# A hybrid decoder step: all low parts of the split weights on DVE, and one more slot in the mLSTM heads between the power and the row scaling

## Chip, cores and metric

One core of a Trainium2 chip. The metric is the time of one execution on the device in microseconds (us), as the median of several runs. All times below are of the core's engines as the hardware profiler recorded them: PE (TensorE, matrix products; PEld its weight loads), DVE (VectorE), ACT (ScalarE), POOL (GpSimd) and SP (SyncE, which issues DMAs).

## The reference, cut to what matters

One layer of a decoder runs on 512 prompt tokens and 64 sample tokens (8 sequences of 8), with a width of 1024 and fp32 throughout:

```
hn = rmsnorm(x) * (1 + sc1) + sh1                      # adaLN from c
u  = hn @ w_in
z, xbc, dt, q, k, v, o, ig, fg, xr, gr = split(u)
y_ssd = rmsnorm(ssd_chunked(silu(conv(xbc)), softplus(dt), ...) * silu(z))
y_ml  = rmsnorm(mlstm_chunked(q, k, v, ig, log_sigmoid(fg))) * sigmoid(o)
y_lru = lru_scan(...) * gelu(gr)
x  = x + g1 * (concat(y_ssd, y_ml, y_lru) @ w_out)
h2 = rmsnorm(x) * (1 + sc2) + sh2
x  = x + g2 * (relu(h2 @ w_up)**2 @ w_down)
y  = rmsnorm(x)                                         # and 14 state outputs
```

`ssd_chunked` goes through 128-token chunks of 16 heads in two groups; `mlstm_chunked` does the same for 4 heads and ends in `num / max(|den|, exp(-m))`, whose rows are then RMS-normalised per head.

## The kernel before

The 576 tokens are the free axis of every product, in two halves of 288. The weights are cut into 125 blocks of 1024 x 128. So that fp32 products can be made of three faster ones, each block is split as it arrives: a high part `wh`, the weight rounded to fp32r by ACT (L150), and a low part `wl`, the raw weight minus the high part (L152). The activations are split likewise, and `mm_k` (L164) makes hi x hi, hi x lo and lo x hi for two halves and eight k: 48 products of about 0.13 us, some 6.4 us of PE per block. Blocks have buffers for three raw tiles, three high and three low parts (`RAW_BUFS`, `W_BUFS`); raw tiles are loaded four blocks ahead and split two blocks ahead (`LOOKAHEAD`, `PREP`).

Which engine makes the low part is set by `WL_POOL`: blocks 7 to 32 on POOL, all others on DVE. In the trace POOL's 26 start between 68.0 and 345.6 us. The products of a block gather in a PSUM slot (`pg`, two slots); an evacuation follows, which for the twelve conv blocks (`ev_conv`, L605 to L653) is: ACT copies the sums into a row buffer `r` (L611 to L614; four such buffers), ACT and DVE do the four taps (L620, L626), ACT a tanh (L649), and DVE the gate into `xbc` (L651, L653), which also ends the use of the row buffer.

Between the blocks runs everything else, as Python generators: the gate rows, two SSD groups (`ssd`), four mLSTM heads (`mlstm`), the RG-LRU, the adaLN rows, the gates. `unit` gives each generator in `active` a step (`slot()`) after every four of a block's eight k, which is every 24 products, and after its end. A `yield` therefore means "the next instructions are written one slot later". The order of blocks is written out (`ORDER`: conv blocks c9 c11 c4 c5 c6, mLSTM head m0, c7, m1, m2, then z, x, g and o blocks, m3 late). The order in which each engine finally gets its instructions is not this order: the framework's scheduler reorders the program by a simulated timeline, so that another engine for one instruction moves others on every engine.

In an SSD chunk, L688 to L691 make `cb` and `xt` on PE, DVE makes `cbm` (L693), `xdt` and `xend` (L698) and `att` (8 x L707, ACT's exp, 2 x L711), and PE makes `py` (L729, from the second chunk on also L732) and the state product `ps` (L734). DVE then writes y from `py` (4 x L736). In an mLSTM head, `mlstm` ends with column work: DVE to L1053, the power -1/2 on POOL (L1054), a product (L1056) and the scaling of five row tiles `num` (L1059); after a slot PE transposes them into `pt` (L1063, L1064), and ACT copies them out.

Of the kernel before, what the change touches and what calls it, by code (L numbers as in the profile page):

```python
# [22 lines left out]
FT = mybir.dt.float32  # L23
# [3 lines left out]
OP = mybir.AluOpType  # L27
# [40 lines left out]
class Kernel:  # L68
# [63 lines left out]
    def w_prep(self, upto):  # L132
        nc = self.nc
        while self.w_next_split <= min(upto, NBLK - 1):
            b = self.w_next_split
            self.w_load(b)
            raw = self.w_raw.pop(b)
            m = raw.shape[2]
            if b == 0:
                self.w_split[b] = raw  # L140
            elif b == 3:
                hl = [[self.T("wt", FR)[:, :512].rearrange("p (k m) -> p k m", k=4) for _ in range(2)] for _ in range(2)]
                for (hi, lo), src in zip(hl, (raw[:, :4], raw[:, 4:])):
                    nc.scalar.activation(hi, src, AF.Copy)
                    nc.vector.tensor_tensor(lo, src, hi.bitcast(FT), op=OP.subtract)
                self.w_split[b] = (lambda k, t=hl: t[k // 4][0][:, k % 4], lambda k, t=hl: t[k // 4][1][:, k % 4], m)
            else:
                hi = self.wpool.tile([128, 8, m], FR, name=self.name("wh"), tag="wh", bufs=W_BUFS)
                lo = self.wpool.tile([128, 8, m], FR, name=self.name("wl"), tag="wl", bufs=W_BUFS)
                nc.scalar.activation(hi, raw, AF.Copy)  # L150
                eng = nc.gpsimd if b in WL_POOL else nc.vector
                eng.tensor_tensor(lo, raw, hi.bitcast(FT), op=OP.subtract)  # L152
                self.w_split[b] = (lambda k, t=hi: t[:, k], lambda k, t=lo: t[:, k], m)
            self.w_next_split += 1

# [749 lines left out]
    def mlstm(self, h, q, k, v):  # L905
        nc, io = self.nc, self.io
# [145 lines left out]
        nc.vector.tensor_tensor(ss, ss, r2, op=OP.mult)  # L1052
        nc.vector.tensor_scalar(ss, ss, 1.0 / 128, EPS, op0=OP.mult, op1=OP.add)  # L1053
        nc.gpsimd.tensor_tensor(r2, ss, self.mhalf, op=OP.pow)  # L1054
        fac = cp()
        nc.vector.tensor_tensor(fac, den, r2, op=OP.mult)  # L1056
        for c in range(5):
# [422 lines left out]
W_BUFS = 3  # L1480
RAW_BUFS = 3
CONV = "addd"
WL_POOL = range(7, 33)
ON_POOL = ('fin', 's0', 'S', 'rmax', 'gu1', 'gu2', 'cf2', 'vm')
TAIL = 2, 1, 2

# [152 lines left out]
```

## Time and profile before

| what | value |
|---|---|
| median of 3 runs | 996.15 us (993.74, 996.48, 996.15) |
| the profiled execution | 995.4 us, of which its span 993.6 us |
| mean granted clock of PE | 0.987 |
| PE busy | 959.5 us, 97% of the span |
| DVE busy | 590.2 us, 59% |
| ACT busy | 399.8 us, 40% |
| POOL busy | 203.8 us, 21% |

The profile is of one execution, and its times are counted from the span's start. A group of instructions is told by its line, its engine, its operation and its tiles, `out<-in`. A wait is put down to the instruction that ended it, as in "PE g L164 <- ACT r L614". A matrix product's row gives how long it took with its neighbours overlapping it, so that one of 0.13 us is shown with more. The clock column of a stretch is the clock that PE was granted there, 1.00 being full speed.

### The profile page before, as it was taken

The page shows a single profiled execution, that of the slowest core. Times are in us where ns is not written, and L with a number is a line of the kernel's source. Part 1 is how long each engine was busy: PE and PEld are TensorE (multiplying, and loading weights), DVE is VectorE, ACT ScalarE, POOL GpSimd, SP SyncE. Part 2 cuts the span into 40 slices and gives each one's busy share as a digit, 9 for nine tenths or more (in the row PEclk, how much of TensorE's full clock was granted, in tenths as well). Part 3 has the DMA queues.
Part 4 walks back from the last instruction along what each step waited for, and adds up shares of the span by engine and source line. Part 5 has one row for each costly group of instructions (what it writes and reads, how often), then busy time and mean ns, then how long its engine had stood idle before and what let it go on. Part 6 is the DMA issues. An engine that isn't in the chain of part 4 may idle for free.

```text
span 993.6 us, 18146 instructions
## 1 busy us (share of the span) xinstructions
PE 959.5 (97%) x7369; PEld 904.1 (91%) x7370; DVE 590.2 (59%) x1180; ACT 399.8 (40%) x741; POOL 203.8 (21%) x220
## 2 busy tenths in 40 slices
PE   8999789889999999999999999999999999999996
PEld 5889778777788899999999999999999999999996
DVE  4669897887788377468444455533553355335544
ACT  3454744453646674345222234312441144114320
POOL 2836454532355532020000000000000000000032
PEclk8999999998999999999999999999999999999998
DMA  9721254654464333444222322222222222222202
GB/s 343 294 86 64 81 186 133 246 173 137 131 223 153 105 137 129 140 131 162 91 98 105 110 86 84 74 79 84 85 86 85 86 85 76 76 83 85 85 23 96
DMA packets 51220, 119.62 MB, mean 120 GB/s; under 512 B 6956, under 2 KB 17468, under 8 KB 51136
## 3 DMA queue, kind: packets, MB, share of 16 engines
q1 hardware_dynamic: 47024, 111.06, 32.7%
q10 hardware_dynamic: 3744, 6.85, 1.8%
q8 instruction: 58, 0.95, 0.4%
q0 software_dynamic: 368, 0.55, 0.2%
q14 instruction: 26, 0.21, 0.1%
HBM read 108.68 MB, written 9.76 MB: 119 GB/s over the span
## 4 chain that ended last, share of the span: by engine, by line
PE 76%; DVE 10%; ACT 4%; issue 3%; DMA 1%; POOL 0%; POOLq 0%; DVEq 0%; ACTq 0%
PE g L164 66%; DVE r L626 3%; PE adap L218 1%; PE g L1363 1%; DMA nmb<-scr_nm 1%; PE py L729 1%; PE lg L1129 1%; DVE att L707 1%; PE ps L734 1%; PE py L732 1%; DVE nmb L924 1%; DVE xbc L651 0%; DVE sp_e L494 0%; PE adas L228 0%; ACT r L620 0%
## 5 line engine op out<-in xcount | busy, mean ns | idle before, releaser
L150 ACT ACTIVATE wh<-raw 128x1024 fp32r<-128x1024 f32 x123 | 130.1, 1058 | 333.9 <-PE g L164 309.4
L164 PE MATMUL g<-hnh,wh 128*128 128x288 f32 x688 | 153.1, 302 | 10.1 <-ACT r L614 8.0
L164 PE MATMUL g<-hnh,wl 128*128 128x288 f32 x688 | 152.1, 299 | 0.6 <-DVE wl L152 0.6
L164 PE MATMUL g<-hnl,wh 128*128 128x288 f32 x688 | 151.8, 299 | 0.0
L152 DVE TENSOR_TENSOR wl<-raw,wh 128x1024 fp32r<-128x1024 f32 x97 | 118.7, 1225 | 29.5 <-ACT wh L150 29.4
L164 PEld LDWEIGHTS g<-hnh,wh 128*128 128x128 f32 x688 | 110.4, 189 | 19.3 <-ACT r L614 9.2
L164 PEld LDWEIGHTS g<-hnh,wl 128*128 128x128 f32 x688 | 111.6, 189 | 2.7 <-issue 1.2
L164 PEld LDWEIGHTS g<-hnl,wh 128*128 128x128 f32 x688 | 111.7, 189 | 0.8 <-issue 0.4
L164 PE MATMUL g<-h2h,wh 128*128 128x288 f32 (+1 forms) x512 | 110.9, 297 | 0.0
L164 PE MATMUL g<-h2l,wh 128*128 128x288 f32 (+1 forms) x512 | 110.9, 298 | 0.0
L164 PE MATMUL g<-h2h,wl 128*128 128x288 f32 (+1 forms) x512 | 110.0, 296 | 0.0
L307 DVE SCALAR_TENSOR_TENSOR xr<-g,modt,xr 128x288 f32<-128x288 f32 x38 | 19.7, 518 | 141.2 <-PE g L164 141.2
L164 PE MATMUL g<-hh,wl 128*128 128x288 f32 x480 | 102.9, 295 | 0.0
L164 PE MATMUL g<-hh,wh 128*128 128x288 f32 x480 | 102.5, 295 | 0.0
L164 PE MATMUL g<-hl,wh 128*128 128x288 f32 x480 | 102.4, 295 | 0.0
L1405 POOL TENSOR_SCALAR xr<-xr,vec 128x576 f32<-128x576 f32 (+2 forms) x8 | 15.2, 1900 | 383.8 <-ACT sqa L1237 363.4
L152 POOL TENSOR_TENSOR wl<-raw,wh 128x1024 fp32r<-128x1024 f32 x26 | 69.0, 2653 | 80.3 <-ACT wh L150 61.4
L164 PEld LDWEIGHTS g<-h2h,wl 128*128 128x128 f32 x512 | 83.4, 188 | 0.0
L164 PEld LDWEIGHTS g<-h2h,wh 128*128 128x128 f32 x512 | 83.1, 189 | 0.1
L164 PEld LDWEIGHTS g<-h2l,wh 128*128 128x128 f32 x512 | 83.0, 188 | 0.0
L164 PEld LDWEIGHTS g<-hh,wh 128*128 128x128 f32 x480 | 77.0, 188 | 0.0
L164 PEld LDWEIGHTS g<-hh,wl 128*128 128x128 f32 x480 | 77.0, 188 | 0.0
(399 smaller groups left out, 1652.7 us busy)
## 6 DMA issues: line engine op xcount, KB each, us to landing
raw<-w SPq DMA_DIRECT2D x124, 512.0 KB, 3.5
ada<-ada SPq DMA_DIRECT2D x32, 512.0 KB, 5.6
ada<-ada SPq DMA_DIRECT2D x32, 256.0 KB, 5.9
cumb<-scr_cum SPq DMA_DIRECT2D x16, 256.0 KB, 5.6
s<-s SPq DMA_DIRECT2D x16, 256.0 KB, 4.7
ssm_s<-s ACTq DMA_DIRECT2D x16, 256.0 KB, 2.9
x<-x SPq DMA_DIRECT2D x8, 288.0 KB, 4.7
xr<-x SPq DMA_DIRECT2D x8, 288.0 KB, 3.9
```

The source lines that it names most:

```text
L150: nc.scalar.activation(hi, raw, AF.Copy)
L152: eng.tensor_tensor(lo, raw, hi.bitcast(FT), op=OP.subtract)
L164: self.nc.tensor.matmul(pg.h[h][:m, :e], w(k), xx[:, h * HALF:h * HALF + e], start=start and n == 0, stop=stop and n == 2)
L218: nc.tensor.matmul(ps[32 * j:32 * j + 32, :256], self.cs[:, k, :], ks(k), start=k < 4, stop=k >= 4)
L307: self.nc.vector.scalar_tensor_tensor(dst[:, :HALF], pg.h[0][:, :HALF], gate[:, 0:1], x[:, :HALF], op0=OP.mult, op1=OP.add)
L626: nc.vector.scalar_tensor_tensor(a[:, :n], r[:, j:j + n], wcols[:, j:j + 1], a[:, :n], op0=OP.mult, op1=OP.add)
L707: self.eng("att").tensor_scalar(E[:, h * 128:(h + 1) * 128], cums[h2][:, h * 128:(h + 1) * 128], self.col1[:, c, hd:hd + 1], 0.0, op0=OP.a ...
L729: nc.tensor.matmul(o, xdt[:, h * 64:(h + 1) * 64], att[h // 4][:, hs], start=True, stop=not c)
L732: nc.tensor.matmul(o, S[:, h * 64:(h + 1) * 64], ce[h // 4][:, hs], start=False, stop=True)
L734: nc.tensor.matmul(pst, cb[:, 128:256], xend[:, :512], start=True, stop=True)
L924: self.eng("nmb").tensor_scalar(E[:, tk(c)], nmb[:, tk(c)], ecol(c), 0.0, op0=OP.add, op1=OP.min)
L1405: self.eng("fin").tensor_scalar(x, x, self.v("fnw")[:, o:o + 1], None, op0=OP.mult)
```

## The change

`WL_POOL` is gone: the low part of every block is made on DVE (26 instructions of L152 move from POOL to DVE). In each of the four heads a `yield` stands between the power on POOL and the product and scaling on DVE, so that the latter two are written a slot later, and the transposes with them. Nothing else in the code is changed. In the rows below, the lines 152 to 1053 of the kernel before are one lower; lines 1056 to 1064 are the same.

```
@@ w_prep
                 nc.scalar.activation(hi, raw, AF.Copy)
-                eng = nc.gpsimd if b in WL_POOL else nc.vector
-                eng.tensor_tensor(lo, raw, hi.bitcast(FT), op=OP.subtract)
+                nc.vector.tensor_tensor(lo, raw, hi.bitcast(FT), op=OP.subtract)
@@ mlstm
         nc.gpsimd.tensor_tensor(r2, ss, self.mhalf, op=OP.pow)
+        yield
         fac = cp()
         nc.vector.tensor_tensor(fac, den, r2, op=OP.mult)
@@
-WL_POOL = range(7, 33)
```

The scheduler's new order, at three places. The first is PE's, at the first two chunks of the first SSD group: `py_1434` is the first chunk's product, `py_1563` the second's, and g_1724 is the block of weights between them. Before:

```order
L729 MATMUL py_1434<-att_1372,xdt_1368 64x128 x4
L729 MATMUL py_1434<-att_1379,xdt_1368 64x128 x4
L734 MATMUL ps_1435<-xend_1369,cbm_1365 128x512
...
L691 MATMUL xt_1487<-vec,xbc_1005 128x128
L164 MATMUL g_1724<-hnl_352,wh_1458 128x288 x2
L164 MATMUL g_1724<-hnh_351,wl_1459 128x288 x2
...
L164 MATMUL g_1724<-hnl_617,wh_1458 128x288 x2
L164 MATMUL g_1724<-hnh_616,wl_1459 128x288 x2
L729 MATMUL py_1563<-att_1501,xdt_1497 64x128 x2
```

Between the last xt_1487 and py_1563 stand 40 products of the block. After the change:

```order
L728 MATMUL py_1434<-att_1372,xdt_1368 64x128 x4
L733 MATMUL ps_1435<-xend_1369,cbm_1365 128x512
...
L163 MATMUL g_1724<-hnl_576,wh_1458 128x288 x2
L163 MATMUL g_1724<-hnh_575,wl_1459 128x288 x2
L163 MATMUL g_1724<-hnh_616,wh_1458 128x288
L728 MATMUL py_1434<-att_1379,xdt_1368 64x128 x4
L163 MATMUL g_1724<-hnh_616,wh_1458 128x288
L163 MATMUL g_1724<-hnl_617,wh_1458 128x288 x2
L163 MATMUL g_1724<-hnh_616,wl_1459 128x288 x2
L728 MATMUL py_1563<-att_1501,xdt_1497 64x128 x2
```

The first chunk's py has moved 30 products back (its second half 35), the second's has kept its place behind the end of the block; ten products are left between them, five behind the second half.

The second place is DVE's, between the same two chunks: y from py_1434, and then what makes the operands of py_1563. Before:

```order
L736 SCALAR_TENSOR_TENSOR y_1310<-xbc_1005,vec,py_1434 128x128
L693 TENSOR_TENSOR cbm_1494<-cb_1486,vec 128x128
L698 TENSOR_TENSOR xdt_1497<-xt_1487,col_1216 128x512
L698 TENSOR_TENSOR xend_1498<-xt_1487,col_1216 128x512
L707 TENSOR_SCALAR att_1501<-cumb_1386,col_1216 128x128 x4
L707 TENSOR_SCALAR att_1510<-cumb_1388,col_1216 128x128 x4
L651 SCALAR_TENSOR_TENSOR xbc_1560<-r_1547,r_1553 128x512
L653 SCALAR_TENSOR_TENSOR xbc_1560<-r_1547,r_1553 128x64
L711 TENSOR_TENSOR att_1501<-att_1501,cbm_1494 128x512
```

After:

```order
L735 SCALAR_TENSOR_TENSOR y_1310<-xbc_1005,vec,py_1434 128x128
L692 TENSOR_TENSOR cbm_1494<-cb_1486,vec 128x128
L697 TENSOR_TENSOR xdt_1497<-xt_1487,col_1216 128x512
L697 TENSOR_TENSOR xend_1498<-xt_1487,col_1216 128x512
L706 TENSOR_SCALAR att_1501<-cumb_1386,col_1216 128x128 x4
L706 TENSOR_SCALAR att_1510<-cumb_1388,col_1216 128x128 x4
L650 SCALAR_TENSOR_TENSOR xbc_1560<-r_1547,r_1553 128x512
L652 SCALAR_TENSOR_TENSOR xbc_1560<-r_1547,r_1553 128x64
L151 TENSOR_TENSOR wl_1849<-raw_1590,wh_1848 128x1024
L710 TENSOR_TENSOR att_1501<-att_1501,cbm_1494 128x512
```

The rows are the same but for one low part, wl_1849, which now stands ahead of the last instruction for att_1501. Its high part uses the buffer that the products of g_1724 read to the end.

The third place is PE's, at the transposes of the first mLSTM head (`pt`) and the products of one chunk of the second SSD group (py_2576 before, py_2566 after). Before:

```order
L164 MATMUL g_2665<-hnl_617,wh_2347 128x288 x2
L164 MATMUL g_2665<-hnh_616,wl_2348 128x288 x2
L1063 MATMUL pt_2566<-vec,num_2215 128x128 x3
L1063 MATMUL pt_2566<-vec,num_2216 128x128
L1064 MATMUL pt_432_2567<-vec,num_2216 128x64
L729 MATMUL py_2576<-att_2509,xdt_2505 64x128 x2
L732 MATMUL py_2576<-cumb_2340,S_2432 64x128 x2
...
L732 MATMUL py_2576<-cumb_2342,S_2432 64x128 x2
L734 MATMUL ps_2577<-xend_2506,cbm_2502 128x512
```

After:

```order
L163 MATMUL g_2665<-hnh_616,wl_2348 128x288 x2
L163 MATMUL g_2845<-hnh_297,wh_2527 128x288 x2
L728 MATMUL py_2566<-att_2502,xdt_2498 64x128 x2
L733 MATMUL ps_2567<-xend_2499,cbm_2495 128x512
L163 MATMUL g_2845<-hnl_298,wh_2527 128x288
L731 MATMUL py_2566<-cumb_2340,S_2432 64x128 x2
...
L731 MATMUL py_2566<-cumb_2342,S_2432 64x128 x2
L1063 MATMUL pt_2618<-vec,num_2215 128x128 x3
L1063 MATMUL pt_2618<-vec,num_2216 128x128
L1064 MATMUL pt_436_2619<-vec,num_2216 128x64
```

The transposes, ahead of the chunk's py before, now stand behind it, its ps and three products of the next block.

More of the change, by code (lines that the diff above doesn't have):

```diff
@@ L150, in w_prep @@
                 nc.scalar.activation(hi, raw, AF.Copy)
-                eng = nc.gpsimd if b in WL_POOL else nc.vector
-                eng.tensor_tensor(lo, raw, hi.bitcast(FT), op=OP.subtract)
+                nc.vector.tensor_tensor(lo, raw, hi.bitcast(FT), op=OP.subtract)
                 self.w_split[b] = (lambda k, t=hi: t[:, k], lambda k, t=lo: t[:, k], m)
@@ L1054, in mlstm @@
         nc.gpsimd.tensor_tensor(r2, ss, self.mhalf, op=OP.pow)
+        yield
         fac = cp()
@@ L1482 @@
 CONV = "addd"
-WL_POOL = range(7, 33)
 ON_POOL = ('fin', 's0', 'S', 'rmax', 'gu1', 'gu2', 'cf2', 'vm')
```

## The prediction

> **What bounds the kernel now.** I read the page's totals, then the waits of PE, the stretches, the chain of waits, and the timelines of DVE, POOL and PE where PE stands.
>
> The page first: busy time per engine, then the weights' high parts on ACT and their low parts on DVE and on POOL (busy us, mean ns; idle time before).
>
> ```profile
> span 993.6 us, 18146 instructions
> PE 959.5 (97%) x7369; PEld 904.1 (91%) x7370; DVE 590.2 (59%) x1180; ACT 399.8 (40%) x741; POOL 203.8 (21%) x220
> L150 ACT ACTIVATE wh<-raw 128x1024 fp32r<-128x1024 f32 x123 | 130.1, 1058 | 333.9 <-PE g L164 309.4
> L152 DVE TENSOR_TENSOR wl<-raw,wh 128x1024 fp32r<-128x1024 f32 x97 | 118.7, 1225 | 29.5 <-ACT wh L150 29.4
> L152 POOL TENSOR_TENSOR wl<-raw,wh 128x1024 fp32r<-128x1024 f32 x26 | 69.0, 2653 | 80.3 <-ACT wh L150 61.4
> ```
>
> PE is the bound: it is idle for 993.6 - 959.5 = 34 us in all. The change adds no product, so it can only shorten or lengthen PE's idle time and its time at a lower clock. Three of PE's waits that the terms below use (us in all, times, longest); the long ones stand further down on its timeline:
>
> ```profile
> PE py L729 <- DVE att L711: 2.8, 2, 1.5
> PE pu L829 <- ACT cc L825: 0.7, 1, 0.7
> PE pv L937 <- DVE s L835: 0.6, 1, 0.6
> ```
>
> Stretches (start:end and length, busy us of PE, PEld, DVE, ACT, POOL, then PE's granted clock):
>
> ```profile
> 75.00:100.00 25.00, 24.08 (x181) 23.62 (x179) 24.82 (x31) 11.69 (x22) 15.26 (x18) 1.00 0.20 68
> 125.00:150.00 25.00, 22.20 (x190) 19.35 (x189) 24.96 (x59) 13.08 (x25) 12.61 (x9) 1.00 0.57 183
> 400.00:425.00 25.00, 25.00 (x208) 22.96 (x208) 10.96 (x24) 10.77 (x26) 0.59 (x1) 1.00 0.42 142
> 103.60:107.30 3.70, 3.65 (x17) 3.60 (x17) 3.50 (x8) 3.20 (x4) 0.37 (x2) 0.54 0.05 10
> 225.40:230.30 4.90, 4.85 (x38) 4.16 (x38) 0.68 (x4) 1.26 (x3) 0.00 (x0) 0.52 0.79 211
> ```
>
> DVE has next to no time left where PE stands (24.82 and 24.96 of 25 us); from 400 us on PE is full and DVE is under half. So the case is decided early. The last two stretches are the time behind PE's two long idles: there the clock was about half, which cost 3.70 x 0.46 = 1.7 us and 4.90 x 0.48 = 2.35 us. PE's idles themselves, on its timeline (start, us; idle before it), with the two rows of the last SSD work behind the pt:
>
> ```profile
> 103.65 0.70 PE L164 MATMUL g<-hnh,wh 128*128 128x288 f32 x2 [4.28 <-ACT r L614]
> 113.74 0.53 PE L164 MATMUL g<-hnh,wh 128*128 128x288 f32 x2 [1.36 <-ACT r L614]
> 132.82 1.26 PE L729 MATMUL py<-att,xdt 128*64 128x128 f32 x16 [1.53 <-DVE att L711]
> 142.47 0.44 PE L729 MATMUL py<-att,xdt 128*64 128x128 f32 x4 [1.27 <-DVE att L711]
> 225.45 1.09 PE L1063 MATMUL pt<-vec,num 128*128 128x128 f32 x4 [4.26 <-DVE num L1059]
> 226.76 0.69 PE L729 MATMUL py<-att,xdt 128*64 128x128 f32 x4
> 230.29 1.12 PE L734 MATMUL ps<-xend,cbm 128*128 128x512 f32 x2
> ```
>
> **What a low part costs on either engine.** DVE's timeline between 68 and 137 us has instructions that take about 2 us too long, next to ones of their own kind that do not (the 0.68, 0.83, 0.45 and 1.65 rows); two come from the chain of waits, where they stand alone:
>
> ```profile
> 66.26 0.68 DVE L651 SCALAR_TENSOR_TENSOR xbc<-r,r 128x512 f32<-128x512 f32 x1
> 68.58 2.42 DVE L651 SCALAR_TENSOR_TENSOR xbc<-r,r 128x512 f32<-128x512 f32 x1 [1.50 <-ACT r L649]
> 73.04 5.38 DVE L626 SCALAR_TENSOR_TENSOR r<-r,cwh,r 128x600 f32<-128x600 f32 x4 [0.26 <-ACT r L620]
> 82.57 2.65 DVE L489 TENSOR_TENSOR sp_s<-sp_s,sp_e 128x288 f32<-128x288 f32 x1
> 85.14 0.83 DVE L626 SCALAR_TENSOR_TENSOR r<-r,cwh,r 128x600 f32<-128x600 f32 x1
> 85.90 0.45 DVE L490 TENSOR_TENSOR sp_z<-sp_s 128x288 f32<-128x288 f32 x1
> 107.55 2.81 DVE L626 SCALAR_TENSOR_TENSOR r<-r,cwh,r 128x600 f32<-128x600 f32 x1
> 121.61 2.06 DVE L626 SCALAR_TENSOR_TENSOR r<-r,cwh,r 128x600 f32<-128x600 f32 x1 [0.83 <-ACT r L620]
> 127.25 3.33 DVE L707 TENSOR_SCALAR att<-cumb,col 128x128 f32<-128x128 f32 x8
> 133.29 3.69 DVE L626 SCALAR_TENSOR_TENSOR r<-r,cwh,r 128x600 f32<-128x600 f32 x2
> 139.34 1.65 DVE L707 TENSOR_SCALAR att<-cumb,col 128x128 f32<-128x128 f32 x8
> ```
>
> ```profile
> 91.46 2.56 DVE sp_e L494
> 96.13 2.57 DVE sp L499
> ```
>
> Under each of these nine lies a low part on POOL. One of them:
>
> ```profile
> 82.04 2.86 POOL L152 TENSOR_TENSOR wl<-raw,wh 128x1024 fp32r<-128x1024 f32 x1 [1.55 <-ACT wh L150]
> ```
>
> DVE's L489 began at 82.57, inside POOL's run, and ended at 85.22, just behind POOL's 84.90. So one DVE instruction is held until POOL's is done. The nine excesses over the undisturbed kind are 1.74 + 2.2 + 2.2 + 2.1 + 2.1 + 1.98 + 1.23 + 1.7 + 2.0 = 17.2 us. (For the runs of four and two I took 3.2 and 1.6 us as undisturbed, four and two starts 0.8 apart.) As DVE's own work the nine cost 9 x 1.225 = 11.0 us, so DVE, which is full here, gains 6.2 us. Over all 26 the same count gives about 31 us of holding against 26 x 1.225 = 31.9 us of new work: nothing gained in total, since later DVE is often idle beside POOL.
>
> [...]
>
> **The sum, part by part,** against the profiled 995.4 us (its span is 1.8 us less); the median of the runs, 996.15, is 0.75 above it.
>
> *Idle at 99.4 us.* The block that starts at 103.65 needs its PSUM slot drained by ACT, which needs a conv row buffer that DVE frees. Five holds lie ahead of it: 10.3 us. Five low parts on DVE are 6.1 us. That is 4.2 us less DVE work, but ACT has a high part (1.04 us) ahead of the drain in the new order, and DVE lost 1.50 us idle at 68 us which stays. Walking the new order with these durations I get an idle of 1.9 us for 4.28: **-2.4** (bounds 0 and -4.2). An idle of 1.9 leaves no half clock (it stood after 4.28 and 4.26 alone): **-1.7** (0 if the idle stays over 4).
>
> *Idles to 133 us.* 1.36 becomes about 1.1; the 1.53 hangs on DVE's own rows and goes, as DVE is ahead and PE's order puts 30 more products before the first py: **-1.8** (bounds -1.8 and 0).
>
> *A new idle at the second py (142.47 before).* Of the first SSD group, 40 products of blocks lay between the two chunks before, 10 lie there now (front part on the change): 1.3 us of cover for 5.4. DVE's chain between them, from its timeline:
>
> ```profile
> 136.91 1.11 DVE L736 SCALAR_TENSOR_TENSOR y<-xbc,vec,py 128x128 f32<-128x128 f32 x4
> 141.64 0.68 DVE L711 TENSOR_TENSOR att<-att,cbm 128x512 f32<-128x512 f32 x1
> ```
>
> From 136.91 to 142.32 it takes 5.4 us, and a low part now stands in it, in front of the last row: 6.6. Less 1.3 of products, plus about 0.7 for DVE's arriving late, the idle is 6.0 where it was 1.27: **+4.7**. Bounds: this low part needs ACT's high part, whose slot the last products in front free; that alone is 1.04 + 1.22 + 0.68 = 2.9 us (+1.7), and if DVE comes late as it did before (py's products end at 134.0, DVE starts at 136.91) it is 6.6 - 1.3 + 2.9 = 8.2 (+6.9). Behind it a half clock is to be expected as behind both idles over 4 us: **+1.7** (0 to 2.35, the two rows). Queued behind that waiting DVE chain are the next group's cumb products and xbc; PE waits for all.
>
> *142 to 205 us.* The two waits of 0.7 and 0.6 (cc, s) are hidden by DVE's being ahead: **-1.2** (0 to -2).
>
> *The slot in the heads, idle at 221.19.* Without the yield the scaling by L1059 follows the power at once, in the same slot, and pt follows the scaling. Rows:
>
> ```profile
> 219.15 2.72 POOL L1054 TENSOR_TENSOR col<-col,mhalf 128x5 f32<-128x5 f32 x1 [5.01 <-DVE col L1053]
> 222.98 3.10 DVE L1059 TENSOR_SCALAR num<-num,col 128x128 f32<-128x128 f32 x5
> 222.89 2.33 POOL L152 TENSOR_TENSOR wl<-raw,wh 128x1024 fp32r<-128x1024 f32 x1
> ```
>
> L1059's five are held by the low part at 222.89 (3.10 for about 1.05 us of work, five of eight at 1.65): 2.05 us go. In PE's new order pt stands behind a group's py and ps and 3 products instead of ahead of them: the py took 3.5 us (226.76 to 230.29) at half clock, so 1.8 at full, the ps 1.1 and the products 0.4: 3.3 us later. Together 5.3 us against an idle of 4.26, with one more low part (1.2) on DVE ahead: 0.2 us of idle stays at least, and I take 0.6 for the power. So **-3.7**, and the half clock behind goes: **-2.35**. Bounds: all of 4.26 goes, or the scaling comes a whole slot of 24 products (3.2 us) later by the yield and 3.4 us of idle remain (-0.9, half clock kept: 0). The other three heads' pt lie where PE has products to spare; the yield moves them one slot back, under later blocks: 0.
>
> *After 226 us.* The C load's DMA stands earlier on SP's queue and the products pq may wait for it: **+0.5** (0 to 1.5). From 300 us on PE has no idle to gain and DVE is half empty: 0.
>
> Sum: -2.4 - 1.7 - 1.8 + 4.7 + 1.7 - 1.2 - 3.7 - 2.35 + 0.5 = **-6.25**, so 989.1 on the profiled time and 989.9 against the median; I say 989.9.
>
> **Rivals.** (A) *No new idle at the second py.* If PE's products after the first chunk run later than I think, or DVE is ahead enough, +4.7 + 1.7 falls to 0: about -12.7, 983. For: DVE gains 6 us by then. Against: the chain starts only when py's products are done.
>
> (B) *DVE even, nothing moves.* The total of 31 against 31.9 says so; the early gain would be lost as ACT's drain and the slot of the raw weights set the idle at 99.4. Then the terms are 0 there, +6.4 at py, -6.05 at pt and -1.2 between: about -1, 995.
>
> (C) *Slower: the low part in DVE's order stops PE.* On POOL a low part that waits for ACT's high part waits alone; on DVE every row behind it waits too, and the high part waits for PE's slot. Place: the new idle at the second py. If ACT's high part comes another 3 us late there and the same happens at one more chunk (another 5.4 - 1.3 with its half clock, +6), I get -6.25 + 3 + 6 = +2.8, and with the idle at 99.4 kept (+4.1) +6.9, 1003. It decides from 6.3 us of added waits, and from 9.3 it can be measured. For: 90.8 us of engine time before these low parts are waits for ACT's high part. Against: in the new order they stand mostly where the high part is long done.
>
> [...]
>
> (D) *Each low part on POOL held DVE for its whole length.* Then DVE gains 12.9 us here and not 6.2, since holds lie hidden in its waits too. The 6.7 us more could shorten the idles at 99.4 and at py, by about 1.9 and 2.5: -10.6, 985. For: the held rows all end with POOL's. Against: the nine excesses are counted, and what lies in a wait cost nothing. [...]
>
> **Chances.** Forecast 0.45, A 0.15, D 0.10, B 0.17, C 0.13. A difference of 0.3%, 3 us, is about what a measurement of this kernel can tell. Forecast, A and D are faster save a tenth of the forecast's own spread: 0.66. B and that rest are no change: 0.21. Slower: C, 0.13. The range leaves out half of A and most of C: 983 to 997.
>
> **What the next profile would show.** Right: no L152 on POOL; no stretched DVE rows of the nine; the idle before the block of 103.65 under 2.5 us and no 0.5 clock there; an idle of 3 to 8 us before the second py with DVE att as its releaser; no idle over 1 us before pt. Wrong: an idle over 4 us at the first place still, no idle at the second py, or PE's waits on DVE wl in the page's list above 3 us in all.

## The result, and the profile after

The changed kernel takes 991.72 us (median of 20 runs) against 998.43 us for the kernel before in the same comparison: a ratio of 0.9933, with a 95% interval of 0.9909 to 0.9957. That is 0.67%, or 6.7 us, faster; 6.25 us was forecast. The profiled execution after has a span of 989.9 us, 3.7 us less than before's. Runs of one kernel spread over 13 us here (986.3 to 999.3 after; the last section goes into why), so a single pair of profiles shows where time went and not how much.

The page after, with the totals and the low parts, all on DVE now:

```profile
span 989.9 us, 18136 instructions
PE 959.0 (97%) x7370; PEld 904.9 (91%) x7370; DVE 579.1 (59%) x1206; ACT 400.4 (40%) x741; POOL 134.9 (14%) x194
L151 DVE TENSOR_TENSOR wl<-raw,wh 128x1024 fp32r<-128x1024 f32 x123 | 151.3, 1231 | 43.2 <-ACT wh L150 37.8
```

DVE took over 26 instructions, 151.3 - 118.7 = 32.6 us of work, and its busy time *fell* by 590.2 - 579.1 = 11.1 us. All its other work became 43.7 us shorter. Not all of that is holding by low parts. I compared each DVE row with the median, over all thirteen profiles, of the same instruction's rows without a POOL instruction beside them. In the kernel before, the rows that overlap one of the 26 low parts are 34.5 us longer in all, and those that overlap POOL's other work alone 20.5 us, which is 13.5 us after. So 34.5 of the 43.7 us are the low parts' and 7.0 come from other POOL instructions that now meet DVE less. In no profile is a row more than 0.5 us too long without a POOL instruction beside it. One of the nine rows that the prediction names, which took 2.65 us before, is after:

```profile
82.59 0.44 DVE L488 TENSOR_TENSOR sp_s<-sp_s,sp_e 128x288 f32<-128x288 f32 x1
```

PE's long idles after, on its timeline (the idle in brackets), in the places of those shown of before:

```profile
102.50 0.53 PE L163 MATMUL g<-hnh,wh 128*128 128x288 f32 x2 [1.55 <-ACT r L613]
111.23 0.53 PE L163 MATMUL g<-hnh,wh 128*128 128x288 f32 x2 [1.55 <-ACT r L613]
142.54 0.69 PE L728 MATMUL py<-att,xdt 128*64 128x128 f32 x4 [5.81 <-DVE att L710]
185.11 0.50 PE L828 MATMUL pu<-xst,bst 96*128 96x512 f32 x1 [1.16 <-DVE modt L228]
266.53 0.53 PE L163 MATMUL g<-hnh,wh 128*128 128x288 f32 x2 [1.34 <-ACT v L901]
```

The idle of 4.28 us at the conv blocks is 1.55, the one of 4.26 before pt is gone (no idle over 0.4 us stands from 186 to 261 us), and there is a new one of 5.81 us at the second py. DVE's chain ahead of it, from its timeline:

```profile
135.93 1.12 DVE L735 SCALAR_TENSOR_TENSOR y<-xbc,vec,py 128x128 f32<-128x128 f32 x4 [3.02 <-PE py L728]
136.97 0.28 DVE L692 TENSOR_TENSOR cbm<-cb,vec 128x128 f32<-128x128 f32 x1
137.17 0.68 DVE L697 TENSOR_TENSOR xdt<-xt,col 128x512 f32<-128x512 f32 x1
137.77 0.68 DVE L697 TENSOR_TENSOR xend<-xt,col 128x512 f32<-128x512 f32 x1
138.37 1.65 DVE L706 TENSOR_SCALAR att<-cumb,col 128x128 f32<-128x128 f32 x8
139.93 0.68 DVE L650 SCALAR_TENSOR_TENSOR xbc<-r,r 128x512 f32<-128x512 f32 x1
140.53 0.22 DVE L652 SCALAR_TENSOR_TENSOR xbc<-r,r 128x64 f32<-128x64 f32 x1
140.67 1.22 DVE L151 TENSOR_TENSOR wl<-raw,wh 128x1024 fp32r<-128x1024 f32 x1
141.81 0.69 DVE L710 TENSOR_TENSOR att<-att,cbm 128x512 f32<-128x512 f32 x1
```

It starts when the first py ends and runs without a break for 6.6 us. Two stretches, the one behind the new idle and one of the early time, with the granted clock as the third figure from the end:

```profile
142.50:147.70 5.20, 5.16 (x25) 3.46 (x27) 3.61 (x7) 0.82 (x2) 1.06 (x1) 0.52 0.75 202
75.00:100.00 25.00, 25.00 (x191) 25.00 (x190) 24.03 (x38) 13.84 (x25) 4.33 (x14) 1.00 0.26 85
```

Behind the new idle the clock was half, as expected: 5.16 x 0.48 = 2.5 us. From 75 to 100 us DVE is as full as before (24.03 us of 25, 24.82 before), but PE is no longer idle there (25.00 us busy, 24.08 before).

**Where the time went, by stage.** PE's order keeps the block products in their order in all kernels, so they serve as marks: the start of product 192, 480, 864, 1056 and 2112 of the 5856. Between two marks I add up PE's gaps, and half of its busy time at a clock of 0.5. All in us:

| stage, in products | before: length, idle, clock | after: length, idle, clock | length after less before |
|---|---|---|---|
| 192 to 480 (conv blocks) | 46.8, 5.9, 1.7 | 42.2, 3.1, 0 | -4.6 |
| 480 to 864 (first SSD group) | 100.9, 6.5, 0 | 101.9, 7.0, 2.5 | +1.0 |
| 864 to 1056 (pt, second SSD group) | 58.3, 6.3, 2.35 | 53.4, 2.9, 0 | -4.9 |
| 1056 to 2112 | 193.3, 1.5, 0 | 195.1, 2.0, 1.7 | +1.8 |
| sum | 399.2, 20.2, 4.05 | 392.5, 15.0, 4.2 | -6.6 |

What lies outside the marks differs by +2.9 us in this pair. Of it 2.3 us is more idle of PE before 49 us (5.96 against 3.64), which the second profile of the kernel after hasn't got (3.51). Half clock costs about the same ahead of product 192 in both (4.9 and 5.0 us): the one at 62 us that only the kernel after has (last section) is made up by one fewer before 49 us. The rest, 0.7 us behind product 2112, is not explained. The runs' times, not this pair, say what the change is worth.

### The profile page after: what moved, and what is told of

It reads as the page before. It is cut to its first block, busy times and chain, and to the rows that moved or that the text cites. A ratio compares the mean times of both kernels' runs of the same rounds, so it can differ in the third digit from the quotient of the medians.

```text
span 989.9 us, 18136 instructions
## 1 busy us (share of the span) xinstructions
PE 959.0 (97%) x7370; PEld 904.9 (91%) x7370; DVE 579.1 (59%) x1206; ACT 400.4 (40%) x741; POOL 134.9 (14%) x194
## 4 chain that ended last, share of the span: by engine, by line
PE 84%; DVE 4%; ACT 3%; DMA 2%; issue 1%; POOL 0%; POOLq 0%; DVEq 0%; SPq 0%; ACTq 0%
PE g L163 73%; PE adap L217 1%; PE g L1363 1%; PE ps L733 1%; PE py L728 1%; DMA nmb<-scr_nm 1%; PE py L731 1%; DMA ada<-ada 1%; DMA cump<-scr_cum 0%; PE lg L1129 0%; PE xt L690 0%; PE adas L227 0%; DVE wl L151 0%; PE pu L828 0%; PE pn L970 0%
## 5 line engine op out<-in xcount | busy, mean ns | idle before, releaser
L151 DVE TENSOR_TENSOR wl<-raw,wh 128x1024 fp32r<-128x1024 f32 x123 | 151.3, 1231 | 43.2 <-ACT wh L150 37.8
L163 PE MATMUL g<-hnh,wh 128*128 128x288 f32 x688 | 155.6, 304 | 9.7 <-ACT r L613 5.2
L163 PEld LDWEIGHTS g<-hl,wh 128*128 128x128 f32 x480 | 76.9, 188 | 0.0
L1405 POOL TENSOR_SCALAR xr<-xr,vec 128x576 f32<-128x576 f32 (+2 forms) x8 | 15.2, 1904 | 384.8 <-ACT sqa L1237 364.4
```

The costliest lines, as they stand in the source:

```text
L151: nc.vector.tensor_tensor(lo, raw, hi.bitcast(FT), op=OP.subtract)
L163: self.nc.tensor.matmul(pg.h[h][:m, :e], w(k), xx[:, h * HALF:h * HALF + e], start=start and n == 0, stop=stop and n == 2)
L1405: self.eng("fin").tensor_scalar(x, x, self.v("fnw")[:, o:o + 1], None, op0=OP.mult)
```

## The experiments

The theory: low parts on POOL hold DVE, and taking them off frees DVE; the early gain is in part given back at the second py for want of cover, and the rest comes at pt from both parts of the change. The rivals: the yield alone does it; DVE comes out even; the early blocks, where DVE is full, carry it all.

**One part at a time: the low parts without the yield.** The kernel before with `WL_POOL = ()`, run twice.

```
-WL_POOL = range(7, 33)
+WL_POOL = ()
```

> All low parts on DVE, no yield in the heads. My theory (the early gain comes from DVE's not being held, the gain at pt from both parts): the early terms and the new idle of about 6 us at the second py are all there; at pt, which stands ahead of the chunk's py as before, 2.05 us of holding and about 1.5 us of a slow power go and one low part of 1.2 us comes, so an idle of about 2 us without half clock: about 1.5 us slower than both parts together, some 5 us (0.5%) faster than before. Rival (the yield alone makes the gain, DVE is even): no faster than before, ratio 1.000, and an idle of over 4 us at pt.

> All low parts on DVE, no yield, once more, to see whether it is faster than with the yield. My theory by the traces (idle and half clock from 67 to 466 us are the same with and without it to 1 us): ratio 0.991 to 0.995, as with both. Rival (the yield costs some us): 0.991 or less again.

Measured: 0.9908 (0.9877 to 0.9938) and 0.9915 (0.9888 to 0.9941). The idles at the conv blocks and the second py are those of the kernel after (1.55, 1.55, 5.81). pt, which stands ahead of the chunk's py here, in the first of the two:

```profile
221.85 0.83 PE L1063 MATMUL pt<-vec,num 128*128 128x128 f32 x4 [1.70 <-DVE num L1059]
```

So 2.56 us of the 4.26 go by the low parts alone; 2 us of idle had been expected. The rival falls: the low parts make the whole gain, and more than I allowed them. Whether the yield costs something on top is not settled. The twelve runs without it average 988.0 us, the 32 of the kernel after 992.2, so it may cost some us; but they were taken in different comparisons, whose intervals overlap, and no stage shows the price: between the marks the profiles have 393.0 and 392.9 us without it, 392.5 and 391.8 with it.

**The yield alone.** `WL_POOL` stays.

```
         nc.gpsimd.tensor_tensor(r2, ss, self.mhalf, op=OP.pow)
+        yield
```

> The yield alone, blocks 7 to 32 on POOL as before. My theory: pt goes behind the chunk's py and ps (3.3 us later), so an idle of at most 1 us is left of 4.26 and the half clock behind it goes: 5 to 6 us (0.55%) faster than before; the idles at 99 and 131 us stay as before, and none of 6 us comes at the second py. Rival (the scaling comes a slot later and eats up what the new place gives): idle of 3 us or more at pt and a ratio of 1.000. Rival (it is all in DVE's share): ratio 1.000 with the idle gone.

Measured: 1.0001 (0.9978 to 1.0024). My theory is wrong here. What came is what the second rival said, a ratio of 1.000 with the idle gone: the idle at pt is gone without a rest, but others have come up behind it. PE's rows:

```profile
237.39 0.44 PE L732 MATMUL py<-cumb,S 128*64 128x128 f32 x4 [1.02 <-DVE cumb L716]
263.13 0.41 PE L1018 MATMUL pj<-ci,vec 128*32 128x130 f32 x4 [0.93 <-ACT ci L1010]
266.55 1.06 PE L822 MATMUL pc<-s,xbc 128*32 128x512 f32 x8 [1.69 <-issue]
268.92 0.47 PE L829 MATMUL pu<-xst,bst 96*128 96x512 f32 x1 [0.56 <-DVE c L1029]
270.72 0.85 PE L164 MATMUL g<-hnh,wh 128*128 128x288 f32 x2 [1.34 <-ACT v L902]
```

From product 864 to 1056 the idle is 5.65 us against 6.3 before. My reading, which no run isolates, is that the work around pt was late by other ways too, so that PE now waits for the next piece of it. A half clock follows the last of these (1.7 us). Of the 6 us that the step gave to pt's idle, about 1 is left between product 864 and 2112 (250.5 us against 251.5).

**More holding.** The kernel after, with POOL making the low parts of blocks 7 to 32 a second time, into a tile that is not read (the ghost kernel below).

```
                 nc.vector.tensor_tensor(lo, raw, hi.bitcast(FT), op=OP.subtract)
+                if 7 <= b < 33:
+                    gh = self.wpool.tile([128, 8, m], FT, name=self.name("gh"), tag="gh", bufs=1)
+                    nc.gpsimd.tensor_tensor(gh, raw, hi.bitcast(FT), op=OP.subtract)
```

> The kernel after, and POOL makes the low parts of blocks 7 to 32 as well, into a tile that nobody reads (extra work that the output doesn't need). My theory (a POOL low part holds a DVE instruction): DVE's busy time grows by 30 to 44 us against the kernel after, by 17 us between 60 and 140 us where DVE is full, and the run is 8 to 15 us slower than the kernel after, slower than before. Rival (the long rows were waits of another kind, POOL's work beside DVE's costs nothing): as the kernel after, within 2 us, DVE's busy time the same.

Measured: 1.0165 (1.0133 to 1.0198) against the kernel before, 21 us slower than the kernel after. Its page and three of its DVE rows:

```profile
PE 965.1 (96%) x7369; PEld 906.6 (90%) x7370; DVE 614.2 (61%) x1206; ACT 400.4 (40%) x741; POOL 213.7 (21%) x220
```

```profile
73.83 2.98 DVE L628 SCALAR_TENSOR_TENSOR r<-r,cwh,r 128x600 f32<-128x600 f32 x1
77.87 0.83 DVE L628 SCALAR_TENSOR_TENSOR r<-r,cwh,r 128x600 f32<-128x600 f32 x1
82.84 2.64 DVE L491 TENSOR_TENSOR sp_s<-sp_s,sp_e 128x288 f32<-128x288 f32 x1
```

DVE does the same 1206 instructions and is busy 614.2 - 579.1 = 35.1 us longer; the long rows are back (2.98 beside 0.83 us for the same form, and 2.64 for the row of 0.44 above). That POOL's low parts hold DVE is shown: no other work was added. From 60 to 140 us DVE is busy 76.5 us against 67.9, 8.6 more where I expected 17; it had hardly more time there, and PE came to 502 products and not 542. The price was more than I gave: between the marks idle grew by 15.2 us and the loss by half clock by 5.9. Not all of that need be holding: the second low part also reads the raw tile and the high part, whose buffers come free later, and the scheduler's order changes with it; the shares are not shown. The conv blocks' idles are 2.31, 1.82 and 5.37 us here.

**Which blocks.** Low parts of blocks 7 to 16, and of 17 to 32, on DVE alone, without the yield (`WL_POOL = range(17, 33)` and `range(7, 17)`).

> No yield; low parts of blocks 7 to 16 on DVE, of 17 to 32 on POOL as before. My theory: all that the part on DVE gains up to 180 us is here (idle of 1.5 us at 100, 5.8 us at the second py): -4.6 +1.6 = -3 us; pt at 221 keeps the kernel before's idle of about 4 us with half clock. 2 to 4 us faster than before, ratio 0.997. Rival (the whole gain of the part on DVE comes from the early blocks, where DVE is full): ratio 0.991.

> No yield; low parts of blocks 17 to 32 on DVE, of 7 to 16 on POOL as before. My theory: up to 180 us as the kernel before (idles 4.28, 1.4, 1.5, 1.3, none of 6); at pt the idle falls from 4.26 to about 1.7 us and the half clock behind it is halved: 3 to 5 us faster than before, ratio 0.996. Rival (late low parts are hidden, nothing gained): ratio 1.000.

Measured: 1.0004 (0.9977 to 1.0031) for the early blocks and 0.9961 (0.9935 to 0.9988) for the late ones. The early blocks gain nothing that can be measured, less than I expected: the theory's 0.997 lies just outside the interval. PE in their profile:

```profile
138.30 0.70 PE L729 MATMUL py<-att,xdt 128*64 128x128 f32 x4 [5.80 <-DVE att L711]
```

```profile
225.07 1.09 PE L1063 MATMUL pt<-vec,num 128*128 128x128 f32 x4 [4.24 <-DVE num L1059]
```

The 4.6 us won in the conv blocks are there to a tenth (42.1 us from product 192 to 480, as after), but the first SSD group takes 6.4 us longer than before, with 5.3 us lost by half clock, 3.4 of them behind idles of 0.49 and 0.69 us near 191 us that the kernel after hasn't got. With the late blocks alone it is the reverse: the conv blocks are as before (4.30 us idle), there is no long idle at the second py, and pt waits 1.72 us, as expected:

```profile
101.63 0.79 PE L164 MATMUL g<-hnh,wh 128*128 128x288 f32 x2 [4.30 <-ACT r L614]
218.46 0.83 PE L1063 MATMUL pt<-vec,num 128*128 128x128 f32 x4 [1.72 <-DVE num L1059]
```

Between the marks the late blocks alone take 393.0 us, as much as all on DVE (393.0). That pair is not typical, though. The profile of the late blocks is of an execution of 989.82 us, where the median of the twelve is 995.71, and the one of all on DVE is of 992.05 us, the longest of its six (median 987.25). By the runs the late blocks alone seem to make about half of the gain: 0.9961 against 0.9908 and 0.9915, or 994.5 against 988.0 us as the average of twelve runs each, with intervals that overlap a little. Then the early blocks, worth nothing alone, add to it once the late ones are on DVE too. So the rival that the early blocks carry it all is wrong, and so was the weight that I gave to the time in which DVE is full: what is freed there can be spent on the next wait. Why the two parts would do more together than apart is not shown.

**The chain at the second py.** Three kernels. First, all low parts on DVE but block 16's (`WL_POOL = (16,)`, no yield), the one that stands in the chain.

> No yield; all low parts on DVE but that of block 16, the one in DVE's chain ahead of the second py. Orders of PE and DVE up to there are the same but for it. My theory (a POOL low part holds one DVE instruction for 1.2 to 2.2 us where DVE runs without a break): the idle of 5.8 us stays at 5.6 to 6.8 us, since the 1.2 us taken out come back as holding. Rival (off DVE it costs nothing): 4.6 us.

Measured: an idle of 6.10 us (0.9929, 0.9896 to 0.9961). PE's row, POOL's and DVE's:

```profile
146.23 0.70 PE L729 MATMUL py<-att,xdt 128*64 128x128 f32 x4 [6.10 <-DVE att L711]
```

```profile
141.05 2.34 POOL L152 TENSOR_TENSOR wl<-raw,wh 128x1024 fp32r<-128x1024 f32 x1 [2.01 <-ACT wh L150]
```

```profile
141.76 3.08 DVE L707 TENSOR_SCALAR att<-cumb,col 128x128 f32<-128x128 f32 x8
145.50 0.68 DVE L711 TENSOR_TENSOR att<-att,cbm 128x512 f32<-128x512 f32 x1
```

The low part left DVE and took 3.08 - 1.65 = 1.43 us as holding, for 1.2 us of work: at one place, with nothing else changed ahead of it, the two prices side by side. Second, with all low parts on DVE and no yield, y of the first chunk is made behind the att of the second.

In this excerpt `put_y` holds the four instructions that stood at the removed lines.

```
+            if c == 1 and g == 0:
+                put_y()
             if c < 3:
                 cums = [self.ssd_cum(g, c + 1, h) for h in range(2)]
...
-            for i in range(4):
-                nc.vector.scalar_tensor_tensor(ys[i][:, tok], xs[i][:, tok], ...
+            late = c == 0 and g == 0
+            def put_y(tok=tok, py=py):
...
+            if not late:
+                put_y()
```

> All low parts on DVE, no yield, and y of the first group's first chunk is made on DVE behind the att of the second chunk and not ahead of it. My theory (the idle at the second py is DVE's chain from the end of the first py: y, cbm, xdt, xend, att): the chain starts with xt's products, about 1.2 us before the second half of py ends, so the idle of 5.8 us falls to 4.6 to 5.0, a half clock still stands behind it, and the time is 0.5 to 1.5 us less than with all on DVE. Rival (the low part of block 16 or its high part sets the end): 5.8 us.

Measured: an idle of 4.35 us, a little below the 4.6 to 5.0 expected:

```profile
146.54 0.70 PE L731 MATMUL py<-att,xdt 128*64 128x128 f32 x4 [4.35 <-DVE att L711]
```

The ratio is 0.9939 (0.9910 to 0.9968), no change that can be told from all on DVE, and not the small gain that was expected. That the chain starts at the first py and its parts set the idle is shown. Third, one more slot ahead of the second py, in the kernel after.

```
                 cums = [self.ssd_cum(g, c + 1, h) for h in range(2)]
             yield
+            if c == 1 and g == 0:
+                yield
```

> The kernel after, with one more yield in the first SSD group ahead of the second chunk's py. In the new order 53 products of blocks lie between the first chunk's py and the second's instead of 10: about 7 us of cover for DVE's chain of 6.6 us. My theory: the idle of 5.8 us and the half clock behind it (2.6 us) go, 5 to 8 us faster than the kernel after, if nothing later waits for the SSD group's end. Rival (the idle only moves, since the chunks behind wait for the second one): the same idle at the third chunk or at the group's end, within 2 us of the kernel after.

Measured: 1.0033 (1.0007 to 1.0058) against before, so about 1% slower than the kernel after. The idle at the second py is gone and my forecast is wrong by its sign: SSD and mLSTM work now comes later, and with it small idles, of which these are three in a row:

```profile
189.35 0.66 PE L938 MATMUL pv<-vec,v 128*128 128x128 f32 x4 [1.30 <-DVE nmb L932]
190.96 0.50 PE L830 MATMUL pu<-xst,bst 96*128 96x512 f32 x1 [0.34 <-ACT v L948]
192.41 0.79 PE L830 MATMUL pu<-xst,bst 96*128 96x512 f32 x1 [0.95 <-DVE s L836]
```

All idles between the marks are 16.35 us, 1.4 more than after, but three half clocks of 6.8 us each follow such groups of short ones, so that the clock costs 9.1 us where it cost 4.2. The rest of the 9.8 us (392.5 to 402.4) is not explained; this profile is of an execution of 1004.79 us, where the median is 999.35.

**A version between.** POOL makes the low parts of blocks 11 to 16 alone (`WL_POOL = range(11, 17)`, no yield).

> No yield; POOL makes the low parts of blocks 11 to 16 alone, DVE all others. In the new order the first SSD chunk's py stands at product 588 (614 with all on DVE, 584 before), so 36 products lie between it and the second py, 4.8 us of cover instead of 1.3. My theory (the early low parts on DVE gain 4.6 us at 99 us and give most of it back at the second py, for want of cover): the idle at 99 to 105 us is about 2.3 us (one POOL low part is left ahead of it), that at the second py 2 to 3 us, the late part as with all on DVE: 8 to 10 us faster than before, 2 to 3 faster than all on DVE without yield. Rival (it is the holding by POOL's low parts of blocks 11 to 16 between 95 and 140 us that matters): the gains of all on DVE are lost here, ratio 0.996 as for late blocks alone.

Measured: 0.9936 (0.9911 to 0.9961), the same as all on DVE within the intervals and not the 2 to 3 us less that were expected. The idle at the second py is 0.39 us, better than expected; but the conv blocks have 1.91 and then 3.91 us:

```profile
104.16 0.64 PE L164 MATMUL g<-hnh,wh 128*128 128x288 f32 x2 [1.91 <-ACT r L614]
116.78 0.53 PE L164 MATMUL g<-hnh,wh 128*128 128x288 f32 x2 [3.91 <-ACT r L614]
143.81 0.44 PE L729 MATMUL py<-att,xdt 128*64 128x128 f32 x4 [0.39 <-DVE att L711]
```

POOL's low parts hold DVE there again: ahead of the idle of 3.91 us, DVE's L513 and L551 take 3.17 and 2.14 us beside a low part, where the kernel before has 0.51 and 0.16. The three idles are 6.2 us here and 8.9 with all low parts on DVE (1.55, 1.55 and 5.81), so most of the idle has moved and not gone. It was expected that both places would be good at once, and that failed. Between the marks this profile has 390.1 us, 2.9 less than with all on DVE, which the runs don't confirm. No version tried is measurably faster than all low parts on DVE without the yield (0.9908 and 0.9915).

**The kernel after once more.**

> The kernel after once more, unchanged, to see what of it is chance. In its first profile a half clock stood behind an idle of 2.10 us at 59 us, where the same idle in the kernel before brought none. My theory: PE's granted clock goes by fixed stretches of 3.41 us; one with about half of it idle or more (1.6 us and up) is followed by half clock, so the same idles bring or don't bring it by where the grid falls. Then this run has its idles at the same places within 0.3 us (1.55, 1.55, 5.8 before 140 us, none over 1 us at pt), but half clocks partly elsewhere, and a ratio of 0.990 to 0.996. Rival (idle length alone decides): half clocks at the same places as in the first profile.

Measured: 0.9935 (0.9912 to 0.9959), the first measurement again. The main idles are at the same places (1.55, 1.57, 5.81, none over 0.4 at pt). The one of 1.16 us at 185 us is not there, and one at 262 us has 1.55 us instead of 0.61; the half clock at 62 us is gone, which the last section takes up.

## Why the prediction was right, point by point

**The sum.** -6.25 us forecast, -6.7 measured, -6.6 between the marks of the profile pair. That the total came within half a microsecond is in part luck: single terms were off by more than 1 us, both ways. By place it stands so:

- *Idle at the conv blocks and the clock behind it*: -2.4 and -1.7 forecast, 4.28 to 1.55 (-2.7) and -1.7 measured. Right, and the ghost kernel shows the reason, holding.
- *1.36 and 1.53*: the second went as forecast; the first became 1.55 instead of 1.1.
- *The new idle at the second py*: 6.0 forecast, 5.81 measured, with the chain of 6.6 us and the low part in it as put; half clock +1.7 forecast, +2.5 measured, since the idle reached into two clock stretches (3.41 us of it in one, 1.89 in the next).
- *142 to 205 us*: -1.2 forecast, from the waits on cc and s. Both went, but the one on s stands at 292 us in the trace before and not here: the forecast read its place wrong. What went here besides cc was not in the forecast, 0.85 us on C and a part or all of the 1.73 on modt (1.16 after, none over 0.4 us in the second profile of the kernel after). From product 624 to 864 PE is idle for 3.45 us before, 1.16 and 0.18 after. With late blocks alone the idle between products 576 and 864 falls by 2.6 us. So this term was too small.
- *pt*: -3.7 and -2.35 forecast, -4.26 and -2.35 measured there. The size is right and the reason half wrong. The step put 3.3 us down to pt's new place, so to the yield. The runs show that the low parts alone take 2.56 us away, and that the yield alone takes all 4.26 away but gives most of it back within 50 us: its ratio is 1.0001. The gain that is left at the end belongs to the low parts.
- *After 226 us*: +0.5 forecast; +1.8 us from product 1056 to 2112, nearly all a half clock at 267 us behind idles of 0.56 and 1.34. The forecast had a late DMA in mind, which is not what came.

The clock terms at the conv blocks and at pt were right in size, but the reading behind them, half clock after idles of over 4 us alone, was not: in the last section an idle of 2.10 us brought it.

**DVE's balance.** The step that set about 31 us of holding against 31.9 us of new work came close for the low parts themselves: 34.5 us by the rows of the kernel before, 35.1 in the ghost kernel, against 32.6 us of new work. That DVE's busy time fell by 11.1 us and not by about 2 comes mostly from POOL's other instructions, which held it for 20.5 us before and 13.5 after; the forecast did not count them, and why they meet DVE less was not tested. Had each of POOL's 26 low parts held DVE for the whole of its mean 2.65 us, that would be 69 us (an estimate from the page of the kernel before); the rows' 34.5 are half of it. The rest may lie where DVE was waiting anyway, or where its instruction came after the low part's start; that is an inference, not shown.

**The rivals.** A (no new idle) is excluded by the row at 142.54. B had DVE's balance of low parts nearly right (34.5 against 32.6 us), but the idle at the conv blocks went all the same, and its 995 us, a ratio of 0.999, lies outside the interval. C's mechanism is there, DVE's order behind a low part, but at its small price. D's holding for the whole length (9 x 2.65 = 23.9 us at the nine rows, less 11.0 of work: its 12.9) is not there: 34.5 of 69 us.

## What to carry to other kernels

Before moving an elementwise operation to the slower engine beside DVE (here a low part took 2.65 us on POOL and 1.23 on DVE), look for DVE rows of one form with two durations: the long ones tell what the neighbour costs, and the work may be cheaper on the busier engine (here 32.6 us of work against 34.5 of holding). What this frees where an engine is full is not the gain; follow the new order to the next wait, since here 4.6 us won in one stage were given back in the next when the early blocks alone were moved, and the late blocks were needed for any gain. A step that is moved so that nobody waits for it has gained nothing until the next steps of the same chain are shown to be in time: the yield took away an idle of 4.26 us, and the time stayed the same to 0.2%.

## What the runs showed of the hardware

**Half clock came without a long idle.** The same idle of 2.10 us, before the same block at 59 to 61 us, brought no half clock in the kernel before and one of 3.4 us in the kernel after. PE's row after, with the stretch behind it:

```profile
61.08 0.54 PE L163 MATMUL g<-hnh,wh 128*128 128x288 f32 x2 [2.10 <-ACT r L613]
```

```profile
62.40:65.80 3.40, 3.40 (x17) 3.40 (x16) 3.37 (x5) 1.64 (x4) 0.23 (x1) 0.54 0.00 0
```

And the stretch behind the same idle in the kernel before, whose product came at 60.51 us, and in the kernel after's second profile, at 62.69:

```profile
60.50:66.00 5.50, 5.50 (x41) 5.50 (x42) 4.47 (x6) 3.15 (x6) 0.62 (x4) 1.00 0.01 3
```

```profile
62.70:69.00 6.30, 6.30 (x47) 6.30 (x48) 5.29 (x7) 3.15 (x6) 0.61 (x4) 1.00 0.01 3
```

All half clocks lay on a grid of 3.41 us, the length of the shortest: in the kernel after they begin at 14.36, 31.42, 62.14, 140.65 and 266.94 us, which are 5, 9, 23 and 37 such steps apart. Where the idle fell whole into one stretch of the grid (after: 2.10 us of it), half clock followed; where it fell into two (1.19 and 1.03 us of idle before, 1.10 and 1.12 the second time, a gap of 0.12 beside it counted in), none did. I laid that grid over PE's idles in all thirteen profiles, from 50 to 480 us, and counted the stretches at full clock by the idle in them: with 1.8 us or more 28 of 29 were followed by half clock, with 1.6 to 1.8 us 5 of 8, with 1.0 to 1.6 us 2 of 51, with 0.6 to 1.0 us none of 50. Several short idles in one stretch added up: 0.56 and 1.34 us at 264 to 267 us did it in the kernel after. So in these profiles about half of a stretch idle was enough. The grid also goes far to explain why runs of one program differ by 13 us, as each stretch at half clock cost up to 1.7 us (3.41 us at a clock of 0.50). Executions of the kernel after with a mean clock of 0.992 had spans of 984.5 and 984.8 us, those with 0.985 from 989.1 to 990.4, and one with 0.978 had 996.9: a clock lower by 0.014 over 990 us is 14 us, and the spans differ by 12. That it is the grid's place that differs from run to run is seen in the two profiles of this kernel; the other executions have no trace.
